# Moving the split weights and the lo halves of the FFN's middle tiles by 64 bytes

## The chip, the cores and the metric

The kernel runs on one core of one Trainium2 chip. The metric is the device time of one execution in microseconds. Three runs of the kernel before took 1136.83, 1136.86 and 1137.74 us; the median is 1136.86 us.

## The reference

One decoder layer over 512 tokens of width 1024, in float32, made of four sub-layers with a residual add after each and an RMS norm ahead of each:

```python
h = rmsnorm(x, ffn1_norm);  x = x + 0.5 * (silu(h @ w_gate) * (h @ w_up)) @ w_down     # 1024 -> 2816 -> 1024
h = rmsnorm(x, mix_norm);   z = h @ w_in                                              # 1024 -> 2560
#   first 1024 columns: gelu, then gated by 8 causal 128x128 position mixings per chunk (mixer A)
#   last 1536 columns: q, k, v of 8 heads, rotary, three dilated causal windows mixed (mixer B)
x = x + concat(rmsnorm(y_a), rmsnorm(y_b)) @ w_out                                    # 1024 -> 1024
h = rmsnorm(x, cross_norm); x = x + cross_attention(h, rmsnorm(mem))                  # wq, wk, wv, wo: 1024 x 1024
h = rmsnorm(x, ffn2_norm);  x = x + 0.5 * (silu(h @ w_gate) * (h @ w_up)) @ w_down
return rmsnorm(x, final_norm)
```

## The kernel before

Activations are held transposed, as tiles of 128 features by 512 tokens. Every large product is computed in the float32r type, to keep float32 precision, as three matmuls: an operand `a` is split into a rounded part `aH` and the rest `aL`, and `mm3` (lines 124 to 129) issues `aH*bH`, `aH*bL` and `aL*bH` into the same accumulator. The first operand of `mm3` is the stationary one (it is loaded into the array by a LDWEIGHTS), the second is the moving one that streams past. Every MATMUL has its own LDWEIGHTS, also where the stationary tile stays the same.

Weights come from HBM a tile at a time. `load_weight` (lines 109 to 118) issues one DMA from SyncE into `wraw`, has ScalarE round it into `whi` (line 103) and VectorE subtract the two into `wlo` (line 104); each of the three has three buffers in the pool `wp`. In the FFNs, `w_out`, `wq`, `wk` and `wo` the weights are stationary. In the blocks of `w_in` and `wv` it is the other way: slices of the activation are stationary, and the weights move.

An FFN (`ffn`, line 214) runs its 22 column tiles of 128 in two chunks of 11. For each tile it computes gate and up (24 matmuls each), then `evacuate` multiplies them out and splits the result into `hidH` and `hidL`, a tile of 128 by 512 each, with twelve buffers. After a chunk the down product has `whi`, `wlo` stationary and `hidH`, `hidL` moving: `hidH`, `hidL`, `hidH` in turn. In the last chunk of the second FFN the tokens are taken in two halves of 256, and six of eight down weights are kept for the second half in tiles named `wk` of the pool `hp`.

TensorE's order is the program's order; VectorE, ScalarE and SyncE follow in the order that the Tile framework's scheduler gives, each waiting on semaphores. Nothing in the program sets an address: a pool begins where the one opened before it ends, and its tiles lie one behind the other. So a small pool is a way to shift what follows. Line 72 is such a one: the pool `fill` holds one tile of 56 floats and takes the pools behind it from byte 6,944 to byte 7,168 of each partition, which is 56 times 128. Every tile behind it has a length that is a multiple of 512 bytes, up to a few small ones in the mixers, and so in the kernel before the operands of matmuls begin at a multiple of 128 bytes: `hH`, `hL` and all else in `hp` from 37,376 on, `wraw` at 119,296, `whi` at 131,584, `wlo` at 143,872, `hidH` at 168,448 and `hidL` at 193,024, each and its further buffers at 0 modulo 512.

Of the kernel before, what the change touches and what calls it, by code (L numbers as in the profile page):

```python
# [17 lines left out]
F32 = mybir.dt.float32  # L18
F32R = mybir.dt.float32r
# [5 lines left out]
P = 128  # L25
S = 512
# [16 lines left out]

FILL = 56


G_FFN1, G_MIX, G_CROSS, G_MEM, G_FFN2, G_FIN, G_OA, G_OB, G_BS = (
    0, 8, 16, 24, 32, 40, 48, 52, 56)
# [6 lines left out]
def body(tc, I, out):  # L55
    nc = tc.nc
    from contextlib import ExitStack
    ctx = ExitStack()
    with ctx:
# [3 lines left out]
        base = ctx.enter_context(tc.tile_pool(name="base", bufs=1))  # L63
        hp = ctx.enter_context(tc.tile_pool(name="hp", bufs=40))
        wp = ctx.enter_context(tc.tile_pool(name="wp", bufs=3))
        pacc = ctx.enter_context(tc.tile_pool(name="pacc", bufs=4, space=bass.MemoryType.PSUM))
        paux = ctx.enter_context(tc.tile_pool(name="paux", bufs=4, space=bass.MemoryType.PSUM))

# [33 lines left out]
        def split(hi, lo, src):  # L102
            ins = nc.scalar.activation(hi, src, AF.Copy)  # L103
            nc.vector.tensor_sub(lo, src, f32(hi))  # L104
            return ins
# [2 lines left out]

        def load_weight(src, shape, cuts=1):
            raw = wp.tile([P] + shape, F32, name="wraw", tag="wraw")  # L110
            hi = wp.tile([P] + shape, F32R, name="whi", tag="whi")
            lo = wp.tile([P] + shape, F32R, name="wlo", tag="wlo")
            step = shape[0] // cuts
            for c in range(cuts):
                p = slice(c * step, (c + 1) * step if c < cuts - 1 else shape[0])
                last["dma"] = nc.sync.dma_start(raw[:, p], src[:, p])
                last["hi"] = split(hi[:, p], lo[:, p], raw[:, p])
            return hi, lo
# [94 lines left out]

        def ffn(norm, gate, up, down, nxt, first=None, between=None):
            h = (norm.H, norm.L)
            with tc.tile_pool(name="ffn", bufs=2) as fp:
                R = None

                def down_tile(d, w, hid, tok, jj, acc=None, js=range(CF)):
# [21 lines left out]
                def evacuate(ps, hid):  # L241
                    gp = fp.tile([P, S], F32, name="gp", tag="gp")
                    nc.vector.tensor_mul(gp, ps[0], R)  # L243
                    s = fp.tile([P, S], F32, name="s", tag="s")
                    nc.scalar.activation(s, gp, AF.Silu)
                    u = fp.tile([P, S], F32, name="u", tag="u")
                    nc.vector.tensor_mul(u, ps[1], R)  # L247
                    nc.vector.tensor_mul(u, s, u)
                    hH = fp.tile([P, S], F32R, name="hidH", tag="hidH", bufs=12)
                    hL = fp.tile([P, S], F32R, name="hidL", tag="hidL", bufs=12)  # L250
                    split(hH, hL, u)
                    hid[0].append(hH)
                    hid[1].append(hL)
# [3 lines left out]
                for c in range(NCHUNK):  # L257
                    hid = ([], [])
                    for j in range(CF):
                        f = c * CF + j  # L260
                        ps = []
                        for src in (gate, up):
                            if f == 0 and src is gate and first is not None:
                                w = first()
                            else:
                                w = load_weight(src[f], [KD, P])
                            acc = acc_tile()
                            for k in range(KD):
                                mm3(acc, w, h, (slice(None), k), k, k == 0, k == KD - 1)
                            ps.append(acc)  # L270
                            if first is not None and f == 1 and R is None:
                                R = factor()
                        pending.append(ps)
                        if first is not None and f == 0:
                            continue
                        if R is None:
                            R = factor()
                        while pending:
                            evacuate(pending.pop(0), hid)
                    if c < NCHUNK - 1 or nxt is not None:  # L280
                        for d in range(KD):
                            w = [load_weight(down[c, d, :, j0:j1, :], [j1 - j0, P])
                                 for j0, j1 in halves]
                            down_tile(d, w, hid, slice(0, S), halves)
                            if c == NCHUNK - 1:
                                nxt.add(d)
                            elif between is not None:
                                between(d)
                        continue
# [5 lines left out]
                    def weights(d, keep):  # L295
                        if d in kept:
                            return kept[d], thirds
                        if not keep:
                            return [load_weight(down[c, d, :, j0:j1, :], [j1 - j0, P])
                                    for j0, j1 in halves], halves  # L300
                        kept[d] = []
                        for j0, j1 in thirds:
                            raw = wp.tile([P, j1 - j0, P], F32, name="wraw3", tag="wraw")
                            nc.sync.dma_start(raw, down[c, d, :, j0:j1, :])
                            pair = tuple(h_tile("wk")[:, :(j1 - j0) * P]
                                         .rearrange("p (j m) -> p j m", m=P) for _ in range(2))
                            split(*pair, raw)
                            kept[d].append(pair)
                        return kept[d], thirds
# [479 lines left out]
        def between(d):  # L789
            with tc.issue_after(last["dma"].ins):  # L790
                if d == 0:
                    cs.append(rotary_tables(small))
                mem_rows(d)

        ffn(n1, I["gate1"], I["up1"], I["down1"], n2, lambda: w0, between)
        y = mixers(n2, cs[0])
        cross(n3, y, mem["R"], n4)
        ffn(n4, I["gate2"], I["up2"], I["down2"], None)


# [83 lines left out]
```

## Time and profile before

| | |
|---|---|
| median of three runs | 1136.86 us |
| the profiled execution's own time | 1139.12 us |
| its span, from the first instruction to the last | 1137.3 us |
| mean granted TensorE clock | 0.993 |
| instructions | 13932 |
| MATMUL records on PE | 5472 |

The profiled execution is 1.8 us longer than its span and 2.26 us longer than the median of the runs. In the page's rows an engine's name is followed by its busy time, the share of the span and the number of instructions; PE is the matmul side of TensorE and PEld its weight loads, which run beside it. A row of a group names the line, the engine, the operation, what is written and (behind the arrow) what is read, with the moving operand ahead of the stationary one, then the shape, the count, the busy time in us and the mean duration of one in ns, and the idle time before them. In the timeline the first number is the start in us from the span's start, the second the duration. [...]

### The profile page before, as it was taken

The page shows a single profiled execution, that of the slowest core. Times are in us where ns is not written, and L with a number is a line of the kernel's source. Part 1 is how long each engine was busy: PE and PEld are TensorE (multiplying, and loading weights), DVE is VectorE, ACT ScalarE, POOL GpSimd, SP SyncE. Part 2 cuts the span into 40 slices and gives each one's busy share as a digit, 9 for nine tenths or more (in the row PEclk, how much of TensorE's full clock was granted, in tenths as well). Part 3 has the DMA queues.
Part 4 walks back from the last instruction along what each step waited for, and adds up shares of the span by engine and source line. Part 5 has one row for each costly group of instructions (what it writes and reads, how often), then busy time and mean ns, then how long its engine had stood idle before and what let it go on. Part 6 is the DMA issues. An engine that isn't in the chain of part 4 may idle for free. (4 is left out here: it accounts for less than half of the span.)

```text
span 1137.3 us, 13932 instructions
## 1 busy us (share of the span) xinstructions
PE 1121.1 (99%) x5472; PEld 936.4 (82%) x5472; DVE 589.2 (52%) x1023; ACT 422.6 (37%) x668; POOL 66.2 (6%) x82
## 2 busy tenths in 40 slices
PE   9999999999999999999999999999999999999996
PEld 7788888888888888877868988778888888888996
DVE  4544533444344456578797555455444334445542
ACT  6332322332233433567655344433222222233420
POOL 2000100000002000001121000120000000000011
PEclk9999999999999999999989999999999999999998
DMA  6322333222233423010135412132232333323511
GB/s 218 112 93 88 114 97 128 93 93 94 83 88 114 141 93 108 25 45 29 41 111 196 165 63 74 47 102 93 95 99 75 89 125 97 108 93 113 154 63 38
DMA packets 39698, 110.79 MB, mean 97 GB/s; under 512 B 4432, under 2 KB 9296, under 8 KB 39632
## 3 DMA queue, kind: packets, MB, share of 16 engines
q1 hardware_dynamic: 39632, 109.89, 30.1%
q8 instruction: 43, 0.70, 0.2%
q14 instruction: 23, 0.19, 0.1%
HBM read 107.78 MB, written 2.10 MB: 97 GB/s over the span
## 5 line engine op out<-in xcount | busy, mean ns | idle before, releaser
L103 ACT ACTIVATE whi<-wraw 128x1024 fp32r<-128x1024 f32 (+2 forms) x213 | 202.8, 953 | 522.0 <-PE acc L128 300.9
L104 DVE TENSOR_TENSOR wlo<-wraw,whi 128x1024 fp32r<-128x1024 f32 (+2 forms) x213 | 238.4, 1120 | 166.7 <-ACT whi L103 166.4
L127 PE MATMUL acc<-hH,whi 128*128 128x512 f32 x768 | 300.8, 392 | 0.6 <-ACT hH L202 0.6
L128 PE MATMUL acc<-hL,whi 128*128 128x512 f32 x768 | 299.3, 390 | 0.8 <-DVE hL L203 0.8
L129 PE MATMUL acc<-hH,wlo 128*128 128x512 f32 x768 | 299.3, 390 | 0.5 <-DVE wlo L104 0.5
L128 PEld LDWEIGHTS acc<-hL,whi 128*128 128x128 f32 x768 | 144.3, 188 | 31.6 <-DVE hL L203 1.5
L127 PEld LDWEIGHTS acc<-hH,whi 128*128 128x128 f32 x768 | 144.3, 188 | 31.6 <-ACT hH L202 1.0
L129 PEld LDWEIGHTS acc<-hH,wlo 128*128 128x128 f32 x768 | 144.2, 188 | 30.6 <-DVE wlo L104 1.0
L127 PE MATMUL acc<-hidH,whi 128*128 128x512 f32 (+1 forms) x308 | 115.5, 375 | 0.0
L129 PE MATMUL acc<-hidH,wlo 128*128 128x512 f32 (+1 forms) x308 | 115.3, 374 | 0.0
L128 PE MATMUL acc<-hidL,whi 128*128 128x512 f32 (+1 forms) x308 | 115.3, 374 | 0.0
L170 POOL TENSOR_TENSOR sq<-sq 128x512 f32<-128x512 f32 (+1 forms) x39 | 49.3, 1265 | 778.8 <-ACT sq L178 778.4
L247 DVE TENSOR_TENSOR u<-acc,R 128x512 f32<-128x512 f32 x44 | 30.4, 690 | 121.6 <-PE acc L129 121.6
L243 DVE TENSOR_TENSOR gp<-acc,R 128x512 f32<-128x512 f32 x44 | 30.4, 691 | 85.6 <-PE acc L129 81.7
L128 PEld LDWEIGHTS acc<-hidL,whi 128*128 128x128 f32 x308 | 58.0, 188 | 10.3
L127 PEld LDWEIGHTS acc<-hidH,whi 128*128 128x128 f32 x308 | 58.0, 188 | 10.2
L129 PEld LDWEIGHTS acc<-hidH,wlo 128*128 128x128 f32 x308 | 58.0, 188 | 10.2
L127 PE MATMUL acc<-whi,hH 128*128 128x512 f32 x160 | 62.6, 391 | 0.0
L129 PE MATMUL acc<-whi,hL 128*128 128x512 f32 x160 | 62.4, 390 | 0.0
L128 PE MATMUL acc<-wlo,hH 128*128 128x512 f32 x160 | 62.3, 389 | 0.0
L230 DVE SCALAR_TENSOR_TENSOR x<-acc,x 128x512 f32<-128x512 f32 (+1 forms) x40 | 23.3, 584 | 75.0 <-PE acc L129 75.0
L178 ACT ACTIVATE sq<-x 128x512 f32<-128x512 f32 (+1 forms) x48 | 26.0, 551 | 41.8 <-DVE x L230 39.2
(211 smaller groups left out, 1476.6 us busy)
## 6 DMA issues: line engine op xcount, KB each, us to landing
wraw<-up SPq DMA_DIRECT2D x44, 512.0 KB, 3.5
wraw<-gate SPq DMA_DIRECT2D x43, 512.0 KB, 3.4
wraw<-down SPq DMA_DIRECT2D x28, 384.0 KB, 3.1
wraw<-w_in SPq DMA_DIRECT2D x20, 512.0 KB, 3.5
wraw<-down SPq DMA_DIRECT2D x28, 320.0 KB, 2.8
wraw<-w_out SPq DMA_DIRECT2D x16, 256.0 KB, 2.6
wraw<-wv SPq DMA_DIRECT2D x8, 512.0 KB, 3.4
wraw<-wk SPq DMA_DIRECT2D x8, 512.0 KB, 4.0
```

The source lines that it names most:

```text
L103: ins = nc.scalar.activation(hi, src, AF.Copy)
L104: nc.vector.tensor_sub(lo, src, f32(hi))
L127: nc.tensor.matmul(ps, lhsT=aH, rhs=bH, start=start, stop=False)
L128: nc.tensor.matmul(ps, lhsT=aH, rhs=bL, start=False, stop=False)
L129: nc.tensor.matmul(ps, lhsT=aL, rhs=bH, start=False, stop=stop)
L170: nc.gpsimd.tensor_add(self.parts[0], self.parts[0], sq)
L178: nc.scalar.activation(sq, src, AF.Square)
L230: nc.vector.scalar_tensor_tensor(X[d][:, tok], acc, 0.5, X[d][:, tok], op0=ALU.mult, op1=ALU.add)
L243: nc.vector.tensor_mul(gp, ps[0], R)
L247: nc.vector.tensor_mul(u, ps[1], R)
```

## The change

Two pools of one tile of 16 floats (64 bytes) are put around the pool that holds `whi` and `wlo`, which are taken out of `wp` into a pool of their own with the same three buffers. Two more such pools are put around a pool of twelve `hidL` tiles, which is taken out of the FFN's pool and now lies ahead of it. The pad tiles have to be written to be placed, hence a memset of one column for each: two at the start, and two in each FFN. The sizes and numbers of the buffers are as before.

In the allocation of the changed program `wraw` stays at 119,296; `whi` lies at 131,648 and `wlo` at 143,936, which is 64 modulo 128; `hidL` begins at 156,352, 64 modulo 128; the FFN's other tiles follow (`gp` at 180,992, `hidH` at 193,280), and they and all tiles of the mixers and of the cross-attention are at 0 modulo 128, though now at 128 or 256 modulo 512. All of `hp` stays where it was, the `wk` tiles among it.

```diff
+HALF_LINE = 16
...
         wp = ctx.enter_context(tc.tile_pool(name="wp", bufs=3))
+        wpad = ctx.enter_context(tc.tile_pool(name="wpad", bufs=1))
+        ws_ = ctx.enter_context(tc.tile_pool(name="ws", bufs=3))
+        wpad2 = ctx.enter_context(tc.tile_pool(name="wpad2", bufs=1))
+        for pool, n in ((wpad, "pad1"), (wpad2, "pad2")):
+            nc.vector.memset(pool.tile([P, HALF_LINE], F32, name=n)[:, 0:1], 0.0)
...
             raw = wp.tile([P] + shape, F32, name="wraw", tag="wraw")
-            hi = wp.tile([P] + shape, F32R, name="whi", tag="whi")
-            lo = wp.tile([P] + shape, F32R, name="wlo", tag="wlo")
+            hi = ws_.tile([P] + shape, F32R, name="whi", tag="whi")
+            lo = ws_.tile([P] + shape, F32R, name="wlo", tag="wlo")
...
-            with tc.tile_pool(name="ffn", bufs=2) as fp:
+            with tc.tile_pool(name="fpad", bufs=1) as f0, tc.tile_pool(name="fl", bufs=12) as fl, \
+                    tc.tile_pool(name="fpad2", bufs=1) as f1, tc.tile_pool(name="ffn", bufs=2) as fp:
+                for pool in (f0, f1):
+                    nc.vector.memset(pool.tile([P, HALF_LINE], F32, name="fpad")[:, 0:1], 0.0)
...
-                    hL = fp.tile([P, S], F32R, name="hidL", tag="hidL", bufs=12)
+                    hL = fl.tile([P, S], F32R, name="hidL", tag="hidL")
```

On PE, ScalarE, GpSimd and SyncE the instructions stand in the same order with the same waits as before. On VectorE the six memsets are added, and nothing else moves. The one place where a memset has a wait is the end of the cross-attention, where the second FFN's pools open; `oL` there is the lo part of the attention's output for the last two tiles, `xpt` the transposed softmax. Before:

```order
L728 TENSOR_SCALAR xp<-xp,xrz 128x256 [waits DVE_49]
L728 TENSOR_SCALAR xp<-xp,xrz 128x256
L104 TENSOR_TENSOR xpt<-aux,xpt 128x2x256 [waits Activation_49] x2
L104 TENSOR_TENSOR oL<-aux,oH 128x512 [waits Activation_49] x2
L775 TENSOR_TENSOR x_84<-acc,x_84 128x512 [waits PE_49]
L104 TENSOR_TENSOR wlo<-wraw,whi 128x1024 [waits DMAHW2_49,Activation_49]
```

and now (the lines are ten further down in the changed file, or seven near its start):

```order
L738 TENSOR_SCALAR xp<-xp,xrz 128x256 [waits DVE_49]
L738 TENSOR_SCALAR xp<-xp,xrz 128x256
L111 TENSOR_TENSOR xpt<-aux,xpt 128x2x256 [waits Activation_49] x2
L111 TENSOR_TENSOR oL<-aux,oH 128x512 [waits Activation_49]
L226 MEMSET fpad 128x1 [waits DVE_49,PE_49]
L226 MEMSET fpad 128x1
L111 TENSOR_TENSOR oL<-aux,oH 128x512 [waits Activation_49]
L785 TENSOR_TENSOR x_97<-acc,x_97 128x512 [waits PE_49]
L111 TENSOR_TENSOR wlo<-wraw,whi 128x1024 [waits DMAHW2_49,Activation_49]
```

The two memsets have come between the last two `oL`. The value of PE's semaphore that the first of them waits for is the same one for which ScalarE's rounding of the last `oH` waits.

## The prediction

> **What bounds the kernel now.** I read the page's engine table first, then the chain that ended last, then the groups kept apart by shape, then the timeline. The page's first line and its chain:
>
> ```profile
> PE 1121.1 (99%) x5472; PEld 936.4 (82%) x5472; DVE 589.2 (52%) x1023; ACT 422.6 (37%) x668; POOL 66.2 (6%) x82
> ...
> PE 32%; DVE 0%; issue 0%; ACT 0%; DVEq 0%; ACTq 0%
> ```
>
> TensorE is busy for 99% of the span and the chain that ended last is on PE nearly throughout. A change that moves no instruction can gain or lose only by what one matmul costs. The matmuls that read a tile that is moved, and their neighbours, in the groups by shape (moving operand ahead of the stationary one):
>
> ```profile
> L127 PE MATMUL acc<-hH,whi 128*128 128x512 f32 x768 | 300.8, 392 | 0.6 <-ACT hH L202 0.6
> L128 PE MATMUL acc<-hidL,whi 128*128 128x512 f32 x264 | 102.8, 389 | 0.0
> L127 PE MATMUL acc<-whi,hH 128*128 128x512 f32 x160 | 62.6, 391 | 0.0
> L127 PE MATMUL acc<-yH,whi 128*128 128x512 f32 x64 | 27.4, 431 | 0.6 <-DVE yo L619 0.6
> L127 PE MATMUL acc<-oH,whi 128*128 128x512 f32 x64 | 25.3, 395 | 0.0
> L127 PE MATMUL acc<-whi,mH 128*128 128x512 f32 x32 | 12.5, 389 | 0.0
> L128 PE MATMUL acc<-hidL,wk 128*128 128x256 f32 x132 | 37.6, 285 | 0.0
> L127 PE MATMUL acc<-mH,whi 128*128 128x256 f32 x64 | 18.1, 283 | 0.0
> L128 PE MATMUL acc<-hidL,whi 128*128 128x256 f32 x44 | 12.5, 283 | 0.0
> ```
>
> Each stands for a group of three with the same count, one for each product. So 3 x (768 + 264 + 160 + 64 + 64 + 32) = 4056 matmuls of 512 columns read `whi` or `wlo`, and 3 x (64 + 44) = 324 of 256 columns. Their durations overlap; the price of one is the distance between starts. In the gate and up products, from the timeline, the first and the last of 25 starts (24 steps) with one weight load:
>
> ```profile
> 60.40 0.39 PE L127 MATMUL acc<-hH,whi 128*128 128x512 f32 x1
> 60.40 0.19 PEld L128 LDWEIGHTS acc<-hL,whi 128*128 128x128 f32 x1
> ...
> 65.84 0.39 PE L127 MATMUL acc<-hH,whi 128*128 128x512 f32 x1
> ```
>
> (65.84 - 60.40) / 24 = 0.2267 us. For 256 columns, the first and the last of 21 starts:
>
> ```profile
> 639.83 0.28 PE L127 MATMUL acc<-mH,whi 128*128 128x256 f32 x1
> ...
> 642.23 0.28 PE L129 MATMUL acc<-mH,wlo 128*128 128x256 f32 x1
> ```
>
> 2.40 / 20 = 0.1200 us. So 256 columns more cost 106.7 ns, which is 0.417 ns a column, and each matmul pays 226.7 - 213.3 = 13.3 ns besides, whatever its width. There is one stretch at half the granted clock:
>
> ```profile
> 589.00:592.00 3.00, 3.00 (x8) 2.31 (x7) 3.00 (x5) 1.23 (x2) 1.18 (x1) 0.50 0.56 175
> ...
> 589.03 0.63 PE L127 MATMUL acc<-yH,whi 128*128 128x512 f32 x1
> ...
> 592.02 0.63 PE L128 MATMUL acc<-yL,whi 128*128 128x512 f32 x1
> ```
>
> (The column 0.50 of the window's row is the clock.) The seven steps take 2.99 us, 427 ns each: 512 columns at twice 0.417 ns are 427 ns, so there the 13.3 ns are gone. They are not the array's own time, then, but lie in what feeds it, and vanish when it needs its operands half as fast. These 13.3 ns are all that a tile's place could change: 4056 + 324 = 4380 matmuls pay 58 us for it.
>
> **The change part by part.** It removes nothing and moves no instruction. It adds six memsets and changes places.
>
> *The memsets.* A memset of one column is in the trace, and so are the waits into which the new ones fall:
>
> ```profile
> 0.81 0.06 DVE L73 MEMSET pad<- 128x1 f32 x1 [0.81 <-PEq L873]
> ...
> 8.55 0.50 PE L127 MATMUL acc<-hH,whi 128*128 128x512 f32 x1 [0.59 <-ACT hH L202]
> ...
> 718.56 0.69 DVE L104 TENSOR_TENSOR oL<-aux,oH 128x512 fp32r<-128x512 f32 x1 [0.47 <-ACT oH L103]
> ```
>
> Two stand ahead of the memset of `ones`, which the warm-up matmuls wait for: 2 x 0.06 = 0.12 us later. At 8.55 PE waits 0.59 us for `hH`, whose input is still on its way from HBM, so the delay is covered there; without that wait it would cost its 0.12 us. The first FFN's two come while VectorE waits for its first input. The second FFN's two come between the last two `oL`, where VectorE sat idle for 0.47 us until ScalarE had rounded `oH`; the memset waits for the same matmul as that rounding, so it runs in the gap: 2 x 0.06 is under 0.47. Behind it are queued the last `oL` and the first residual adds of `wo`, and neither comes later. Taken: 0, at most 0.12 us.
>
> *VectorE and ScalarE.* The split now reads `wraw` at 0 and `whi` at 64 and writes `wlo` at 64; `hidL` is written at 64 from two sources at 0. Two sources with the same place modulo 512 against one of them in PSUM:
>
> ```profile
> L104 DVE TENSOR_TENSOR hidL<-u,hidH 128x512 fp32r<-128x512 f32 x44 | 30.1, 686 | 5.7 <-ACT hidH L103 5.6
> ...
> L104 DVE TENSOR_TENSOR qL<-acc,qH 128x512 fp32r<-128x512 f32 x8 | 5.5, 683 | 0.0
> ```
>
> 3 ns apart: equal places cost VectorE nothing now, so unequal ones have nothing to give. These engines are busy for 52% and 37% beside a PE that is never short of them but in the `w_out` stage. Taken: 0.
>
> *TensorE.* No row shows an operand that begins at 64 modulo 128, so its price has to be bounded. From below: all 13.3 ns go, for each matmul that it can concern. From above: every stream that begins there pays the same 13.3 ns once more, the only price for the start of a stream that the rows show. Between these I take 0, by the nearest rows, those for other traffic into the same memory at changing places:
>
> ```profile
> 60.00:100.00 40.00, 40.00 (x178) 33.16 (x177) 17.03 (x20) 11.55 (x15) 0.00 (x0) 1.00 0.32 105
> 100.00:140.00 40.00, 40.00 (x178) 33.12 (x178) 22.21 (x34) 14.28 (x23) 5.25 (x4) 1.00 0.33 97
> ...
> 900.00:940.00 40.00, 40.00 (x178) 33.15 (x177) 13.72 (x16) 8.97 (x11) 0.00 (x0) 1.00 0.34 107
> ```
>
> In 40 us PE ran 178 matmuls each time, with VectorE busy for 13.72 to 22.21 us of it, ScalarE for 8.97 to 14.28 and GpSimd for none or 5.25. Those engines run through their tiles at their own pace, so they meet PE's reads at every place modulo 128. If that met with a loss, the second window would hold fewer matmuls than the third.
>
> [...] The three windows agree as far as the other engines go; on PE's two streams against each other no row can decide. [...]
>
> The sum: 1139.12 us for the profiled execution, plus 0 to 0.12, minus 0. The profiled execution stands 2.26 us above the median of the runs, and the change is measured against runs, so the forecast is the median itself: **1136.9 us**.
>
> **The rivals.** *Faster: the 13.3 ns come from weight loads that meet the moving operand.* The timeline's pair at 60.40 shows that the load for the next matmul starts within 0.01 us of the one that streams; both begin at 0 modulo 512, every time. If the two meet in the same part of the memory there, half a line apart would part them. In favour: the 13.3 ns are the same for 512 and 256 columns, as a cost per weight load would be, and are gone at half clock. Against: the two streams do not run at one pace, so a fixed shift moves the point where they meet rather than removing it. The pace of the loads, from four transposes of 128 columns, where the load and not the stream sets the distance:
>
> ```profile
> 713.30 0.60 PE L736 MATMUL aux<-const,xp 128*128 128x128 f32 x4
> ...
> L736 PE MATMUL aux<-const,xp 128*128 128x128 f32 x32 | 4.4, 275 | 0.0
> ```
>
> (0.60 - 0.275) / 3 = 108 ns for 128 columns of weights, where 128 moving columns take 53. The price: streams at 0 under loads at 64, or the reverse, are the 3 x (768 + 160 + 64 + 64 + 32) = 3264 matmuls of 512 columns, 3 x 64 = 192 of 256 columns, and two thirds of the down products with `whi` and `wlo`, 528 + 88 (under `hidL`, itself at 64, the next load is at 64 too), and the 132 that stream `hidL` beside `wk` at 0: 4204 x 13.3 ns = 56 us. All of it gives 1081 us; half, since a shift need not part the streams wholly, 1109.
>
> [...]
>
> *Slower: a moving stream that begins in mid-line fetches one line more.* 13.3 ns at 0.417 ns a column are 32 columns of 4 bytes, 128 bytes. If operands are fetched in lines of 128 bytes, and the start of each stream costs the 13.3 ns because of it, a stream of 2048 bytes that begins at 64 touches 17 lines instead of 16, and pays once more. It concerns the matmuls whose moving operand is at 64: 3 x (160 + 32) = 576 with weights moving, and 264 + 132 + 44 = 440 with `hidL`; 1016 x 13.3 ns = 13.5 us, so 1150.4 us. Stationary operands that begin at 64 would pay under cover: 108 + 13 = 121 ns against 227. Only at 256 columns (120 ns) would 1 ns stand out, 0.3 us over 324. In favour: the size fits 128 bytes exactly. Against: such a fetch could overlap with the stream before it. It decides as soon as one more line costs over 2.3 us / 1016 = 2.2 ns.
>
> *The places have no effect, but a short wait goes another way.* The half-clock stretch of about 6 us follows a wait of 2 us for `wlo` in the `w_out` stage. Should that fall out differently, 13 matmuls at 427 instead of 227 ns are 2.6 us. This is the forecast's own spread rather than a case of its own.
>
> *That the change does not do what it says* I leave out: the allocation has the tiles at 64 modulo 128.
>
> **How the numbers follow.** The forecast has 0.47, the faster case 0.28, the slower case 0.25. A measurement of this kernel cannot tell 0.2%, 2.3 us, from no change. The forecast's own range is 1134.3 to 1139.5, the 2.6 us of the half-clock stretch either way. The range for all cases reaches up past 1150.4 to 1152, and down to 1110, where half of the faster case's gain lies; what is left out is most of that case's stronger half and the slower case with more than one line. Faster 0.28, same 0.46, slower 0.26.
>
> **What would show it.** The distance between starts in the same views of the changed kernel. Right: 226.7 ns in the gate and up products, in the down products and in the `w_in` blocks, 120 ns in the `wk` product, and 178 matmuls in 40 us. Wrong to the fast side: a distance between 213 and 226 ns in the gate and up products, with the down products' `hidL` matmuls left at 227. Wrong to the slow side: 240 ns where `hidL` or the weights move, and 227 elsewhere. The step that fails in either case is the 0 for TensorE. A longer first 9 us, or VectorE idle in front of the second FFN, would show the memsets mis-sized.

## The result, and the profile after

The changed kernel takes 1154.96 us (median; 1154.80 to 1156.95) against 1137.30 us for the kernel before in the same session (1136.83 to 1138.35). The recorded ratio of the runs is 1.0159, with a 95% interval of 1.0146 to 1.0171 (the two medians alone give 1.0155): slower by 17.7 us, where 1136.9 and no change were forecast, and 3 us above the upper end of the range. The profiled execution took 1154.84 us.

The page of the changed kernel, its span, its engines and the engines' shares of the chain that ended last:

```profile
span 1153.0 us, 13939 instructions
...
PE 1138.6 (99%) x5472; PEld 936.5 (81%) x5472; DVE 590.1 (51%) x1029; ACT 422.6 (37%) x668; POOL 66.5 (6%) x82
...
PE 32%; DVE 0%; issue 0%; ACT 0%; DVEq 0%; ACTq 0%
```

The same 5472 matmuls keep TensorE busy 17.5 us longer; VectorE has six instructions more and 0.9 us more, ScalarE's busy time is the same to the tenth. So the time went into the price of a matmul, and the timeline of the gate and up products of the changed kernel shows it, in the first and the last of 25 starts:

```profile
60.45 0.39 PE L134 MATMUL acc<-hH,whi 128*128 128x512 f32 x1
...
66.05 0.39 PE L134 MATMUL acc<-hH,whi 128*128 128x512 f32 x1
```

5.60 / 24 = 0.2333 us from start to start, where it was 0.2267. In the `wk` product, with 256 columns, the first and the last of 13 starts show the opposite:

```profile
648.82 0.28 PE L136 MATMUL acc<-mH,wlo 128*128 128x256 f32 x1
...
650.18 0.28 PE L136 MATMUL acc<-mH,wlo 128*128 128x256 f32 x1
```

1.36 / 12 = 0.1133 us, where it was 0.1200. The windows of the changed kernel that answer to the three of the prediction (behind the window's length stands PE's busy time, with its number of matmuls in brackets):

```profile
60.00:100.00 40.00, 40.00 (x173) 32.34 (x172) 17.42 (x21) 11.40 (x14) 0.00 (x0) 1.00 0.30 95
100.00:140.00 40.00, 40.00 (x174) 32.33 (x173) 21.61 (x33) 14.12 (x22) 5.26 (x4) 1.00 0.34 105
900.00:940.00 40.00, 40.00 (x177) 32.86 (x176) 13.48 (x17) 8.79 (x11) 0.00 (x0) 1.00 0.35 103
```

173 or 174 matmuls in 40 us of gate and up instead of 178, at full clock. The third holds 177: it lies in the down products of the second FFN, at 228.9 ns from start to start there.

Below, *distance* is the time from one matmul's start to the next, averaged over a group, and *d* is where the stationary operand begins minus where the moving one begins, modulo 256 bytes. That 256 is the right period was found only by the experiments; the table uses it so that it need not be read twice. The distances are worked out from the starts of all matmuls of a group in the two traces, with waits left out; in `w_out` that leaves only some 120 of the 192 steps.

| group | matmuls | d now | distance before, ns | after, ns | change, us |
|---|---|---|---|---|---|
| gate, up, `wq` (512 columns) | 2304 | 64 | 226.9 | 233.3 | +14.8 |
| `wo` | 192 | 64 | 227.8 | 233.4 | +1.1 |
| `w_out` | 192 | 64 | 230.3 | 233.3 | +0.6 |
| down, 512 columns | 792 | 64, 128, 64 in turn | 226.8 | 230.2 | +2.7 |
| weights moving (`w_in`, `wv`) | 576 | 192 | 226.9 | 229.1 | +1.2 |
| `wk` (256 columns) | 192 | 64 | 120.0 | 113.5 | -1.2 |
| last chunk's down (256 columns) | 528 | mixed | 119.9 | 118.0 | -1.0 |

The sum is 18.2 us, against 17.7 measured. Nothing is left over for other engines, waits or the memsets. The 230.2 ns of the down products are a mean of two distances, 231.2 and 228.8 ns, to which the section on two rhythms comes back. The two profiled executions differ by less, 15.7 us, partly because the stretch at half clock behind the `w_out` wait happened to last 6.8 us in the trace of before and 3.4 us in the trace after.

### The profile page after: what moved, and what is told of

The parts are those of the page before. It is cut to its first block, busy times and chain, and to the rows that moved or that the text cites. A ratio compares the mean times of both kernels' runs of the same rounds, so it can differ in the third digit from the quotient of the medians.

```text
span 1153.0 us, 13939 instructions
## 1 busy us (share of the span) xinstructions
PE 1138.6 (99%) x5472; PEld 936.5 (81%) x5472; DVE 590.1 (51%) x1029; ACT 422.6 (37%) x668; POOL 66.5 (6%) x82
## 5 line engine op out<-in xcount | busy, mean ns | idle before, releaser
L134 PE MATMUL acc<-hH,whi 128*128 128x512 f32 x768 | 305.3, 398 | 0.0
L135 PE MATMUL acc<-hL,whi 128*128 128x512 f32 x768 | 303.9, 396 | 0.3 <-DVE hL L210 0.3
L136 PE MATMUL acc<-hH,wlo 128*128 128x512 f32 x768 | 303.9, 396 | 0.2 <-DVE wlo L111 0.2
```

Source lines behind the costliest of these rows:

```text
L134: nc.tensor.matmul(ps, lhsT=aH, rhs=bH, start=start, stop=False)
L135: nc.tensor.matmul(ps, lhsT=aH, rhs=bL, start=False, stop=False)
L136: nc.tensor.matmul(ps, lhsT=aL, rhs=bH, start=False, stop=stop)
```

## The experiments

Two questions were open: what about a place costs time (the place of one operand, as in the prediction's mid-line case, or the place of one against the other), and with which period it repeats. Two kinds of kernel answer them: variants of the layer, timed against the kernel before, and small kernels that hold nothing but rows of equal matmuls. The small ones leave the whole layer out and copy `x` to the output, so only the distances in their traces mean anything, not their times. Each of them ran once; where they share a row at 512 columns with both operands at 0, all four have 226.7 ns.

### Places alone

The first small kernel has rows of 40 matmuls with one stationary and one moving operand, each written at a chosen offset. The core of it:

```diff
+        def placed(name, n, off, src):
+            t = base.tile([P, n + 128], F32R, name=name)
+            nc.scalar.activation(t[:, off // 4:off // 4 + n], src[:, :n], AF.Copy)
+            return t[:, off // 4:off // 4 + n]
...
+            for i in range(REP):
+                nc.tensor.matmul(acc[:cols, :n], lhsT=s[:, :cols], rhs=m[:, :n],
+                                 start=i == 0, stop=i == REP - 1)
```

> Not the layer: the kernel copies x to the output and runs rows of 40 equal float32r matmuls, each row with one stationary tile and one moving tile at set places, alone on the chip but for the start. Theory R (what counts is where the weight load stands against the moving operand, modulo 128): with both at 0, or both at 64, 226.7 ns from start to start for 512 columns and 120 for 256; with one at 0 and the other at 64, about 233 for 512 and about 113 for 256; a stationary operand at 128 as at 0. Theory L (an operand that begins in mid-line of 128 bytes pays for one line more, wherever the other is): both at 64 is the slowest, 240 ns or more for 512 columns, and 64 against 0 is slower for 256 columns too. On both, if the 13.3 ns per matmul come from the weight load meeting the stream, a stationary operand of 64 or 32 columns instead of 128 (a shorter load) pays less than 13.3 ns; if they are the start of the moving stream, the same 13.3 ns.

The timeline of this kernel (start, duration of the whole row, operands as moving, stationary, with their offsets as words):

```profile
12.78 9.23 PE L88 MATMUL acc<-mv_zero,st_zero 128*128 128x512 f32 x40
...
49.58 9.49 PE L88 MATMUL acc<-mv_zero,st_sixtyfour 128*128 128x512 f32 x40
...
86.88 9.49 PE L88 MATMUL acc<-mv_zero,st_onetwentyeight 128*128 128x512 f32 x40
...
96.21 4.95 PE L88 MATMUL acc<-mv_zero,st_zero 128*128 128x256 f32 x40
...
115.17 4.70 PE L88 MATMUL acc<-mv_zero,st_sixtyfour 128*128 128x256 f32 x40
...
138.81 9.26 PE L88 MATMUL acc<-mv_sixtyfour,st_sixtyfour 128*128 128x512 f32 x40
147.91 9.32 PE L88 MATMUL acc<-mv_sixtyfour,st_zero 128*128 128x512 f32 x40
...
166.38 9.37 PE L88 MATMUL acc<-mv_zero,st_zero 128*64 128x512 f32 x40
...
184.89 4.71 PE L88 MATMUL acc<-mv_zero,st_zero 128*64 128x256 f32 x40
```

The starts of two rows, divided by 40, or the last 32 steps of a row (after it has settled), give the distance: 226.7 ns with both at 0 and 226.7 with both at 64, 233.3 with the weights at 64 under a stream at 0, and 228.9 the other way round. At 256 columns 120.0 becomes 113.3. So neither operand's own place matters, only the one against the other; and the signs of the changed kernel at 512 and at 256 columns are both here, with no other engine at work. The row at 128 (233.3) was the surprise: 128 is not "the same place". The rows between, from 32 to 112, had 232.0 to 234.3 ns, but offset 16 had 226.7.

The last two rows load 64 columns of weights instead of 128. If the price came from the load taking reads from the stream, it should fall with a load of fewer columns. At 512 columns it does not: 230.1 ns with both operands at 0, more than the 226.7 of a whole load, and 231.7 with 32 columns. At 256 columns it is 113.3 in both.

### Everything at 64

```diff
-FILL = 56
+FILL = 40
```

`FILL` is the width in floats of the pad tile at the start, ahead of everything else. Every tile behind it moves by 64 bytes, and no distance between those tiles changes.

> The kernel before with a pad of 40 floats instead of 56 ahead of all operands, so that every operand of every matmul begins at 64 modulo 128 instead of 0, and none stands otherwise against another than before. Theory R: 1137 us, as before, and 226.7 ns per matmul of 512 columns. Theory L: at least as slow as the change, 1155 us or more, since all moving operands begin in mid-line and not only some.

Measured: 1137.65 us against 1137.17, ratio 1.0000 (0.9991 to 1.0010). The window of this kernel's trace:

```profile
60.00:100.00 40.00, 40.00 (x178) 33.15 (x177) 17.21 (x21) 11.41 (x14) 0.00 (x0) 1.00 0.33 104
```

178 matmuls, as before. A stream that begins at 64 modulo 128 costs nothing by itself: the prediction's slower rival falls as a mechanism.

### One part of the change at a time

The weights' pools and pads without the `hidL` pool:

```diff
+        wpad = ctx.enter_context(tc.tile_pool(name="wpad", bufs=1))
+        ws_ = ctx.enter_context(tc.tile_pool(name="ws", bufs=3))
+        wpad2 = ctx.enter_context(tc.tile_pool(name="wpad2", bufs=1))
...
-            hi = wp.tile([P] + shape, F32R, name="whi", tag="whi")
-            lo = wp.tile([P] + shape, F32R, name="wlo", tag="wlo")
+            hi = ws_.tile([P] + shape, F32R, name="whi", tag="whi")
+            lo = ws_.tile([P] + shape, F32R, name="wlo", tag="wlo")
```

> The change without its part on hidL: whi and wlo at 64, hidL at 0 like hidH. Theory R: gate, up, wq, w_out and wo as in the change, about 233 ns; in the down products of 512 columns all three matmuls now have the load at 64 under a stream at 0, 233 ns each instead of 230 on the mean, 792 x 3 = 2.4 us more than the change: 1157 us. Theory L: the hidL streams no longer begin in mid-line, so the down products get faster than in the change, under 1155 us.

And the `hidL` pool with its pads, the weights left at 0:

```diff
-            with tc.tile_pool(name="ffn", bufs=2) as fp:
+            with tc.tile_pool(name="fpad", bufs=1) as f0, tc.tile_pool(name="fl", bufs=12) as fl, \
+                    tc.tile_pool(name="fpad2", bufs=1) as f1, tc.tile_pool(name="ffn", bufs=2) as fp:
...
-                    hL = fp.tile([P, S], F32R, name="hidL", tag="hidL", bufs=12)
+                    hL = fl.tile([P, S], F32R, name="hidL", tag="hidL")
```

> The change's part on hidL alone: hidL at 64, whi and wlo at 0. Theory R: only the down products differ from before: of 264 matmuls of 512 columns each, those that stream hidL over a load at 0 become slower by 3 to 7 ns, 0.8 to 1.8 us, and some of 256 columns faster by up to 7 ns: 1137 to 1139 us. Theory L: 440 streams begin in mid-line, at most 440 x 7 ns = 3 us, 1138 to 1140 us. This run sizes the part; it does not tell the theories apart by its time.

Weights alone: 1154.77 us, ratio 1.0150 (1.0135 to 1.0165). `hidL` alone: 1140.26 us, ratio 1.0022 (1.0013 to 1.0031). The first window of each, weights alone:

```profile
60.00:100.00 40.00, 40.00 (x174) 32.20 (x173) 17.03 (x21) 11.41 (x14) 0.00 (x0) 1.00 0.30 96
```

and `hidL` alone:

```profile
60.00:100.00 40.00, 40.00 (x178) 33.10 (x178) 17.35 (x21) 11.91 (x15) 0.00 (x0) 1.00 0.32 104
```

The weights carry nearly all of it. The two parts do not add up (17.6 and 3.1 us against the change's 17.7), since both of them shift *d* of the down products. The gate and up products are at 233.3 ns with the weights moved and at 226.9 without. Three sizes missed. With the weights alone moved, the down products were at 228.9 ns, not 233, and the `wk` product was at 117.8 although its operands lie exactly where they do in the changed kernel, which has 113.5. Its matmuls in the kernel with the weights alone moved, the first and the last of 25 starts (2.83 / 24 = 0.1179 us):

```profile
639.84 0.28 PE L136 MATMUL acc<-mH,wlo 128*128 128x256 f32 x1
...
642.67 0.28 PE L136 MATMUL acc<-mH,wlo 128*128 128x256 f32 x1
```

With `hidL` alone moved, more than the 264 matmuls that stream it became slower, for `hidH` lies behind the two pads and came to 128 modulo 256: *d* is 128, 192, 128 in turn, and no down product is left at 0. The 792 down products of 512 columns rose to 231.8 ns: 792 x 5.0 = 4.0 us, less 528 x 2.8 = 1.5 us for the last chunk's 256 columns (119.9 to 117.1 ns), is 2.5 us, with 3.1 measured.

The first miss has its reason in the addresses. The two pads of the weights together are 128 bytes, so `hidH` and `hidL` behind them came to 128 modulo 256 and *d* is 64 - 128, which is 192 modulo 256. The changed kernel's `w_in` blocks, with the weights moving, have the same *d* and the same 229.1 ns, and so has the small kernel's row with the stream at 64 over weights at 0 (228.9).

### The period

The small kernel again, with stationary operands at thirteen offsets from 0 to 512 against a stream at 0.

```diff
-        st = {o: placed("st_" + words[o // 16], P, o, X[1]) for o in range(0, 144, 16)}
+        offs = (0, 8, 16, 24, 128, 192, 256, 320, 384, 448, 480, 496, 512)
+        st = {o: placed("st_" + "abcdefghijklm"[i], P, o, X[1]) for i, o in enumerate(offs)}
```

> Not the layer: the same kind of rows of 40 equal float32r matmuls as before, with the stationary tile at 0, 8, 16, 24, 128, 192, 256, 320, 384, 448, 480, 496 and 512 bytes against the moving one, for 512 and for 256 columns; then a row with the stationary operand in turn at 0 and 64, one with the moving operand in turn at 0 and 64 over a stationary one at 0, and one with the moving operand at 0, 64, 0 over a stationary one at 64 (the order of the changed down products). Theory P128 (only the place modulo 128 counts): 128, 256 and 384 as 0, and 192, 320, 448 as 64. Theory P512 (the place counts modulo the 512 bytes of one weight load): only 512 as 0, all of 128 to 448 about 233 ns for 512 columns. The first theory has against it that a stationary operand at 128 took 233 ns in the first rows. In the row with the stationary operand in turn: if what counts is the load that runs under a stream, the distances alternate or lie between the two prices.

Four rows of this kernel's timeline; `st_a` is at 0, `st_e` at 128, `st_g` at 256, `st_m` at 512:

```profile
11.93 9.23 PE L88 MATMUL acc<-mv_a,st_a 128*128 128x512 f32 x40
...
48.80 9.45 PE L88 MATMUL acc<-mv_a,st_e 128*128 128x512 f32 x40
...
67.25 9.25 PE L88 MATMUL acc<-mv_a,st_g 128*128 128x512 f32 x40
...
122.52 9.23 PE L88 MATMUL acc<-mv_a,st_m 128*128 128x512 f32 x40
```

The distances at 512 columns:

| offset | 0 | 8 | 16 | 24 | 128 | 192 | 256 | 320 | 384 | 448 | 480 | 496 | 512 |
|---|---|---|---|---|---|---|---|---|---|---|---|---|---|
| ns | 226.7 | 230.6 | 233.3 | 231.1 | 232.2 | 228.8 | 226.7 | 233.3 | 232.6 | 228.8 | 233.3 | 226.7 | 226.7 |

256 is as good as 0 and 512, and 128 is not; 320, 384 and 448 repeat 64, 128 and 192. The period is 256 bytes. At 256 columns only the offsets 0, 256 and 512 have 120.0 in this kernel; the others lie between 115.5 and 118.8. That is not firm: in the first small kernel the offsets 112 and 128 had 120.2 and 120.0 too. One row disagrees at 512 columns with the first small kernel: offset 16 gave 226.7 ns there and 233.3 here.

The kernel ends with three rows that mix places. At 512 columns, weights at 0 and 64 in turn under a stream at 0 had 230.0 ns, streams at 0 and 64 in turn over weights at 0 had 230.8, and streams at 0, 64, 0 over weights at 64 had 234.2, more than the mean of its three pairs taken alone (231.1).

In the layer the period was tried twice, with the change's own pools and memsets and pads of 128 and of 256 bytes:

```diff
-HALF_LINE = 16
+HALF_LINE = 32
```

> The change with pads of 128 bytes instead of 64: whi and wlo stand at 0 modulo 128 and 128 modulo 512, hidL at 384 modulo 512; everything else that the change adds (pools, memsets, hidL ahead of the FFN's other tiles) stays. Theory P128: 1137 us, as before. Theory P512: as slow as the change, 1150 to 1156 us, with about 233 ns in gate and up. Should memsets or the new pools be the cause, it is as slow as the change too, but with 226.7 ns per matmul.

```diff
-HALF_LINE = 16
+HALF_LINE = 64
```

> The change with pads of 256 bytes: the same pools, the same memsets and hidL ahead of the FFN's other tiles, with whi, wlo and hidL at 256 modulo 512 and all other operands at 0. If the place counts modulo 256: 226.7 ns in gate, up and down, and 1137 us within 2 us, as before. If only 0 modulo 512 is good, or if something of the change other than the place costs time: 1150 to 1156 us.

With pads of 128 bytes: 1154.43 us, ratio 1.0152 (1.0138 to 1.0165), although every tile is then at 0 modulo 128. Its window:

```profile
60.00:100.00 40.00, 40.00 (x173) 32.41 (x172) 17.92 (x22) 11.42 (x14) 0.00 (x0) 1.00 0.29 93
```

With pads of 256 bytes: 1137.31 us, ratio 1.0001 (0.9992 to 1.0011). Its window:

```profile
60.00:100.00 40.00, 40.00 (x179) 33.10 (x178) 17.08 (x21) 11.63 (x15) 0.00 (x0) 1.00 0.33 105
```

This second kernel has the same new pools, the same six memsets and the same order of work as the change. So none of these costs anything that can be measured, and the place modulo 256 is the whole cause.

### Two rhythms at one place

To see what offset 16 does, and whether `wk`'s two distances are of the same kind, the small kernel ran its rows in an order that comes back to the same place from different ones, and then the same in bf16:

```diff
-            for o in offs:
-                group([st[o]], [mv], n)
+            for o in (0, 64, 128, 64, 16, 64, 0, 16, 128, 16, 0):
+                group(st[o], mv, n)
+        for n in (S, 256):
+            for o in (0, 64, 128):
+                group(bs[o], bm, n)
```

> Not the layer: rows of 40 equal float32r matmuls again, the stationary tile at 0, 64, 128, 64, 16, 64, 0, 16, 128, 16, 0 bytes against the moving one in this order, for 512 and then 256 columns, so that the same place is entered after different places; then six rows in bf16, at 0, 64 and 128, for 512 and 256 columns. Theory of places alone: each place has one price, 64 always 233.3 ns for 512 columns and 113.3 for 256, 16 always the same. Theory of places and history (two or more steady rhythms at a place other than 0, and what ran before picks one): 0 always 226.7 and 120 ns, the others differ from entry to entry, 16 between 226.7 and 233.3 and 64 at 256 columns between 113.3 and 117.7. For bf16: if the extra 13 to 20 ns belong to reading 4 bytes a column, the rows are near 216 and 109 ns at all three places.

From its timeline:

```profile
48.88 9.49 PE L94 MATMUL acc<-mv_a,st_sixteen 128*128 128x512 f32 x40
...
76.61 9.24 PE L94 MATMUL acc<-mv_a,st_sixteen 128*128 128x512 f32 x40
...
117.91 4.88 PE L94 MATMUL acc<-mv_a,st_sixtyfour 128*128 128x256 f32 x40
...
127.36 4.70 PE L94 MATMUL acc<-mv_a,st_sixtyfour 128*128 128x256 f32 x40
...
165.14 8.81 PE L94 MATMUL acc<-mvb_a,stb_zero 128*128 128x512 bf16 x40
173.78 8.80 PE L94 MATMUL acc<-mvb_a,stb_sixtyfour 128*128 128x512 bf16 x40
```

Offset 16 runs at 233.3 ns when it follows a row at 64, and at 226.7 when it follows a row at 0 or the later row at 128. At 256 columns, offset 64 runs at 117.8, 113.3 and 117.8 in its three rows. Each rhythm holds for all 40 matmuls of a row. Offset 0 is the one place that always had the same distance, 226.7 and 120.0, and at 512 columns offset 64 always had 233.3. So a pair of places does not fix the distance alone: at one pair there are two steady rhythms. The rows leave two readings of what selects one: what ran before, or which of the four accumulators a row writes, since those are used in turn and the rows at 117.8 had the first, the row at 113.3 the third. The layer speaks against the accumulators. The eight tiles of the `wk` product go through all four twice, and all eight have 117.8 ns with the weights alone moved, and 113.3 in the changed kernel from the second tile on.

The down products of the changed kernel show the rhythm changing where other matmuls come in between. In both FFNs they take their operands from the same places modulo 256. Three stretches, the first between two groups of other matmuls in the first FFN, the second later in that FFN, the third in the second FFN:

```profile
158.23 0.50 PE L653 MATMUL aux<-ones,mraw 128*128 128x1 f32 x4
...
159.14 0.39 PE L136 MATMUL acc<-hidH,wlo 128*128 128x512 f32 x1
...
173.56 0.39 PE L136 MATMUL acc<-hidH,wlo 128*128 128x512 f32 x1
173.79 0.59 PE L160 MATMUL aux<-dg,ones 128*128 128x256 f32 x2
...
336.26 0.40 PE L134 MATMUL acc<-hidH,whi 128*128 128x512 f32 x1
...
341.81 0.39 PE L134 MATMUL acc<-hidH,whi 128*128 128x512 f32 x1
...
916.55 0.39 PE L134 MATMUL acc<-hidH,whi 128*128 128x512 f32 x1
...
922.04 0.39 PE L134 MATMUL acc<-hidH,whi 128*128 128x512 f32 x1
```

The first has 14.42 us for 63 steps, 228.9 ns, between tiles at 231.2 ns on either side; the second 5.55 us for 24 steps, 231.3 ns; the third 5.49 us for 24, 228.8 ns. So the rhythm changed where a few other matmuls had come in between (four at 158.23 us, two at 173.79), and then held for at least 63 steps. The `wk` product's two distances at the same addresses, 117.8 ns in one kernel and 113.5 in another, would be of the same kind.

In bf16, with half the bytes a column, the distance is 215.8 ns at all three places (109.2 at 256 columns): no effect of the place. No float32r row of 512 columns comes below 226.7 ns.

### A version that takes only the gain

At 256 columns other places are faster, so one can try to move only what streams 256 columns: in the second FFN's last chunk `hidH` and `hidL` lie 64 bytes further on. For that the twelve `hidH` of this FFN become parts of one tile, and the twelve `hidL` of another, ahead of its other tiles; everything else is as before.

```diff
+                if nxt is None:
+                    rows_of = [fp.tile([P, 12 * S + 128], F32R, name=n, tag=n, bufs=1)
+                               for n in ("hidHr", "hidLr")]
...
+                    if nxt is None:
+                        at0 = len(hid[0]) * S + 16 * c
+                        hH, hL = (t[:, at0:at0 + S] for t in rows_of)
```

> The kernel before, with one thing moved: in the last chunk of the second FFN, whose down products all stream 256 columns, hidH and hidL both begin at 64 modulo 512, and the stationary tiles stay at 0. Theory R, with the 113.3 ns that rows of 256 columns took at that distance: 528 matmuls x 6.7 ns = 3.5 us, 1133.5 us or 0.3% under the kernel before. Theory L: 528 streams begin in mid-line, so 1137 us or slower.

Measured: 1136.35 us against 1137.48, ratio 0.9989 (0.9980 to 0.9998). It is the only kernel here below the one before, by 0.1%, with an interval that ends just under 1. Its matmuls of 256 columns went from 120.0 ns to between 117.4 and 118.0, the slower of the two rhythms: 528 x 2.2 = 1.2 us, where 113.3 ns would have given 3.5.

### Which pair counts

In the trace the load for a matmul runs under the stream of the one before: in the kernel before, a matmul starts at 60.40 us, and with it the load of the next one, 0.19 us long, whose own matmul starts at 60.62. Is it a stream and its own weights that must lie alike, or a stream and the weights loaded under it? The small kernel takes both operands from several places in turn, once in step and once shifted by one:

```diff
+            group([0], [0], n)
+            group([0, 64], [0, 64], n)
+            group([64, 0], [0, 64], n)
+            group([0, 64, 128], [0, 64, 128], n)
+            group([0, 64, 128], [64, 128, 0], n)
+            group([0, 64, 128], [128, 0, 64], n)
+            group([64], [0, 192, 0], n)
```

> Not the layer: rows of 42 float32r matmuls, as in the earlier rows of equal ones, with the stationary and the moving operands now taken in turn from several places; x is copied to the output. Each matmul has its own load, and in the trace that load runs under the stream of the matmul before it. Two theories of which pair of operands sets the distance between starts (0: 226.7 ns at 512 columns; other distances modulo 256: 229 to 233). Theory OWN: a stream and its own weights. Theory UNDER: a stream and the weights of the next matmul, which are loaded under it. Rows at 512 columns. (1) one place: 226.7 by both. (2) both operands 0, 64 in turn, in step: OWN 226.7, UNDER (233.3 + 228.8) / 2 = 231. (3) the weights 64, 0 against streams 0, 64: OWN 231, UNDER 226.7. (4) both 0, 64, 128 in turn, in step: OWN 226.7, UNDER about 231.7. (5) weights 0, 64, 128 against streams 64, 128, 0 (each stream at the place of the next weights): UNDER 226.7, OWN about 230. (6) weights 0, 64, 128 against streams 128, 0, 64: both slow, about 230 to 232, unless it is the weights two matmuls ahead that count, then 226.7. (7) weights at 64, streams 0, 192, 0 in turn, as in the changed kernel's down products: (2 x 233.3 + 232.4) / 3 = 233 if each pair keeps its own price, and 230.2 if the order of places itself makes the kernel's 230.2. The last row repeats the first. At 256 columns the same rows: 120.0 where the theory puts the pair at distance 0, 113 to 119 elsewhere.

Its timeline, the first and the last quoted matmul of the second row (40 steps apart), of the third (41 steps) and of the seventh (39 steps):

```profile
24.20 0.40 PE L86 MATMUL acc<-mv_sixtyfour,st_sixtyfour 128*128 128x512 f32 x1
...
33.47 0.39 PE L86 MATMUL acc<-mv_sixtyfour,st_sixtyfour 128*128 128x512 f32 x1
33.70 0.39 PE L86 MATMUL acc<-mv_zero,st_sixtyfour 128*128 128x512 f32 x1
...
43.19 0.39 PE L86 MATMUL acc<-mv_sixtyfour,st_zero 128*128 128x512 f32 x1
...
72.86 0.39 PE L86 MATMUL acc<-mv_onehundredninetytwo,st_sixtyfour 128*128 128x512 f32 x1
...
81.78 0.39 PE L86 MATMUL acc<-mv_onehundredninetytwo,st_sixtyfour 128*128 128x512 f32 x1
```

231.8 ns in step and 231.5 shifted by one. With three places: 229.9 in step, 233.3 and 232.2 shifted by one and by two. No arrangement of changing places comes back to 226.7, so both theories fall: neither one pair alone decides. The seventh row copies the changed kernel's down products, weights at 64 and streams at 0, 192, 0, and has 228.7, not the 233 that its pairs have one by one. That is the rhythm of the second FFN's down products (228.8); with the first FFN's 231.2 the kernel's mean is 230.2. So a mixture of places has a price of its own, not the mean of its parts: this one costs less, and the rows in step cost more (231.8 and 229.9, where each pair alone has 226.7). By it the down products lost 3.4 ns each on the mean where the gate and up products lost 6.4.

## Why the prediction was wrong

**What bounds the kernel** was read rightly: no wait appeared, the order stood, TensorE is 99% busy and the whole difference lies in the distance between starts.

**The memsets at 0 to 0.12 us** hold. In the trace after, the warm-up matmuls start at 1.14 us instead of 1.08 and the first gate product is 0.03 us later:

```profile
1.14 7.68 PE L91 MATMUL warm_ps<-ones 128*128 128x128 f32 x40 [1.14 <-DVE fpad L226]
...
8.58 0.48 PE L134 MATMUL acc<-hH,whi 128*128 128x512 f32 x1
```

The kernel with pads of 256 bytes, which has all six, is at 1.0001.

**VectorE and ScalarE at 0** hold: 590.1 and 422.6 us busy.

**That the 13.3 ns above the columns' time lie in what feeds the array** agrees with the runs, though none of them shows where: the time above 213.3 ns varies with the place of the operands (13.4 ns at 226.7, 20.0 at 233.3), it is 2.5 ns in bf16 (215.8 less 213.3), and it was gone at half clock (427 ns).

**"TensorE. ... Between these I take 0, by the nearest rows" is the step that failed.** The rows were those of other engines: PE ran 178 matmuls in each window, with VectorE busy for 13.72 us of it or for 22.21. That they meet PE's reads at every place was the author's estimate, which no row shows. The changed kernel has the same picture, 173 and 174 matmuls beside 17.42 and 21.61 us, but it says nothing of PE's two streams against each other, as the prediction itself said a paragraph on ("no row can decide"). From there the value should have stayed open rather than been set to 0 with 0.47 behind it. No run shows that 0; the measured value is +6.4 ns for 2304 of the matmuls, +3.4 and +2.2 ns for 1368 others, and +5.6 and +3.0 ns for the 384 of `wo` and `w_out`. The bounds of 13.3 ns either way did hold. In the small kernel, 226.7 against 233.3 ns is a difference made by the place of the weights alone, with no other engine at work.

**The slower rival**, which set the upper end of the range, came out closest in time, 13.5 us of loss against 17.7, but by chance: its mechanism is wrong. It had 240 ns where the weights or `hidL` move and 227 elsewhere. Measured were 229.1 where the weights move and 233.3 where `h` moves over weights at 64, which that case left at 227; and with everything in mid-line there is no loss (1.0000). Its 13.5 us came from 1016 matmuls at 13.3 ns, where the loss lies in all 4056 matmuls of 512 columns that use the weights, at 2.2 to 6.4 ns.

**The faster rival** named the right quantity, the place of the load against that of the stream; that the two meet in the memory, as it says, is not shown. It had the wrong sign at 512 columns. At 256 columns, where it was counted too, the sign was right and the size half of what it said (6.5 of 13.3 ns for `wk`). The objection raised against it, that a fixed shift only moves the point where two streams of different pace meet, is refuted: at 512 columns a fixed 64 gave 233.3 ns in every row with a whole load. Its picture, that equal places collide and shifted ones part, is refuted as well: at 512 columns no place that was tried is better than an equal one modulo 256.

**The unit was wrong.** The prediction counted in lines of 128 bytes, because 13.3 ns are 32 columns of 4 bytes and the change moves by half of 128. The period is 256, and a pad of a whole 128 costs as much as one of 64.

What stays open is the mechanism under the numbers. That the load takes reads from the stream does not fit by itself: a load of half the columns does not make 512 columns cheaper (230.1 ns), though it does 256 (113.3). That one pair of operands decides does not fit either (231.8 and 231.5). Nor is it known by what rule the matmuls before select one of two rhythms, at offset 16, at offset 64 with 256 columns, or in the down products.

## What to carry to other kernels

In float32r, keep the stationary and the moving operands of 512-column matmuls at the same place modulo 256 bytes (226.7 ns here, against 228.8 to 233.3 at 64, 128 and 192), and look at the addresses again after any edit to a pool, since pads of 64 bytes cost this kernel 1.6% without changing the order of a single matmul. Where TensorE is 99% busy, the number to watch is the distance between starts in one stretch of equal matmuls: 0.2267 against 0.2333 us is seen in 25 rows of a timeline. And a price that no row of the profile shows is best measured by itself: one kernel of equal rows gave here in 250 us what the whole layer's trace could not.

## What the runs showed of the hardware that was not expected

- The distance between float32r matmuls depends on the stationary against the moving operand's address modulo 256 bytes: 226.7 ns at 0, 233.3 at 64, 232.2 to 233.3 at 128, 228.8 at 192, for 512 columns. The absolute place had no effect: both operands at 64 have 226.7 ns as both at 0 do.
- The sign turns with the number of columns: at 256 columns equal places have 120.0 ns and most others 113.3 to 118.8 (128 had 120.0 in one kernel and 118.6 to 118.8 in two). Between the two, at 384 columns, it was 173.3 against 176.7 (weights at 64), and at 320 columns 146.7 for both.
- At one and the same pair of places two steady rhythms occur (226.7 or 233.3 ns at offset 16; 113.3 or 117.8 at offset 64 with 256 columns; 228.8 or 231.2 in the changed kernel's down products). In the changed kernel's first FFN it changed from 231.2 to 228.9 and back to 231.2 ns where four and two other matmuls came in between.
- With fewer columns of weights to load, 512-column matmuls were slower: 226.7 ns with 128 columns of weights, 230.1 with 64, 231.7 with 32, all at equal places.
- In bf16 the place made no difference: 215.8 ns at offsets 0, 64 and 128 (109.2 at 256 columns).
